# Low parts of stationary weights 64 bytes further than the activations, mod 512, in a two-layer decoder trunk

## The chip, the cores and the metric

One core of a Trainium2 chip. The metric is the device time of one execution in microseconds; the time given for a kernel is the median of its runs.

## What is computed

Two decoder layers over 256 tokens of width 2048, in float32. Layer 0 mixes with stick-breaking attention, layer 1 with forgetting attention (softmax with cumulative log-forget-gate bias); each has 16 heads of 128, and 4 heads that attend to a memory of 256 vectors. Nearly all arithmetic is in the projections and the feed-forward:

```python
for i in range(DEPTH):                       # DEPTH = 2
    h = _rmsnorm(x, attn_norm[i])
    mem_h = _rmsnorm(mem, mem_norm[i])
    # q, k, v, q_mem = split(h @ w_in); attention; memory attention (mem_h @ w_mem_kv)
    # y = concatenate([o, o_mem]) @ w_out
    x = x + y
    x = x + _conv_ffn(_rmsnorm(x, ffn_norm[i]), ffn_w_up[i], ffn_conv_w[i], ffn_conv_b[i], ffn_w_down[i])
return _rmsnorm(x, final_norm)

def _conv_ffn(h, w_up, conv_w, conv_b, w_down):
    u = h @ w_up                             # 2048 -> 2 * 5632
    # causal depthwise conv of width 3, then split into gate and val
    return (jax.nn.silu(gate) * val) @ w_down
```

## The kernel before

**Splitting.** Activations and weights are float32. Each is split into a high part (rounded to the type `float32r`) and a low part (the rest), and a product is summed from three: high x high, high x low, low x high. Activations are kept transposed, features on partitions, as tiles `xg` (inputs of a block) and `s` (slots for hidden features and heads), 128 x 512: columns 0 to 255 hold the high part of the 256 tokens, 256 to 511 the low part.

**Weights.** They come from memory in chunks of 128 x 1024 (896 in some of the down projection) into one of seven tiles `raw`, issued by the queue SP. `split_chunk` then makes two tiles: `wh`, a cast on ScalarE, and `wl`, the difference `raw - wh` on VectorE. Three pairs of `wh` and `wl` are used in turn (`AHEAD` = 2 chunks ahead of TensorE). `stream` hands out the next chunk's pair and starts later loads and splits.

**Two kinds of jobs.** In a weights-stationary job (`col_job`, and `project` through `colmm`) the weights are loaded into the array, 128 columns at a time, and the activations move through. For each 128 x 128 block of weights that is a wide product, `wh` stationary with all 512 columns of the activation moving (high x high and low x high in one), and a narrow one, `wl` stationary with the 256 high columns:

```python
self.mm(ps, wh[:, s], x, start and i == 0, last)
self.mm(ps[:, :T], wl[:, s], x[:, :T], False, last)
```

Queries, keys, the output projections and the whole feed-forward run so. In a weights-moving job (`row_job`, for values) the activations are stationary and 512 columns of `wh` or `wl` move; `mm3` issues three wide products there.

In the trace a product is written out<-moving,stationary: `acc<-xg,wl` is the narrow product with the low part stationary, `acc<-wh,xg` a weights-moving one. Each matmul has its own weight load, shown on PEld with the same names.

**Order.** The engines' orders are those in which the code issues (class `Ordered`): background work (norms, attention, gates) is cut into steps that `tick` runs after every four weight blocks.

**Places.** `place` puts a blank tile `pad` of 1920 bytes first, so that `xg` begins at byte 18432 of each partition; all tiles of `xg`, `memk`, `memv`, `wh`, `wl`, `s`, `v` begin at a multiple of 512 bytes. So do the 128-column blocks in them (512 bytes each). Constants behind them lie otherwise: `negL`, the triangle of the stick-breaking sums, at 480 mod 512.

Of the kernel before, what the change touches and what calls it, by code (L numbers as in the profile page):

```python
# [7 lines left out]
F32 = mybir.dt.float32  # L8
F32R = mybir.dt.float32r
# [5 lines left out]
P = 128  # L15
# [6 lines left out]
CW = 1024  # L22
SPARE = 7
AHEAD = 2
RAW = 7


# [19 lines left out]
class Ordered:  # L47


    def __init__(self, tc, engine):  # L50
        self.tc, self.engine, self.last = tc, engine, None
# [31 lines left out]
class Trunk:  # L83
# [9 lines left out]
    def __init__(self, ctx, tc, a, out, chunks):  # L93
        self.a, self.out = a, out
        self.KT = a["xT"].shape[1]
        self.NH = a["wq0"].shape[0]
        self.NF = a["wg0"].shape[0]
        self.chunks, self.dry = (chunks, False) if chunks is not None else ([], True)
        if self.dry:
            no = Nothing()  # L100
            self.sp = self.act = self.dve = self.pool = self.pe = no
            self.cp = self.rawp = self.wp = self.padp = self.bigp = self.slots = no
            self.pairp = self.vp = self.sm = self.rp = self.acc = self.zp = self.misc = no
        else:
            nc = tc.nc
            self.sp, self.act, self.dve, self.pool, self.pe = (
                Ordered(tc, e) for e in (nc.sync, nc.scalar, nc.vector, nc.gpsimd, nc.tensor))
            pool = lambda n, b, **k: ctx.enter_context(tc.tile_pool(name=n, bufs=b, **k))
            psum = dict(space=bass.MemoryType.PSUM)
            self.padp = pool("pad", 1)  # L110
            self.bigp = pool("big", 1)
            self.wp = pool("w", 1)
            self.slots = pool("slots", MH + max(self.NH, self.KT) + SPARE)
            self.vp = pool("v", 1)
            self.pairp = pool("pair", 3)
            self.rawp = pool("raw", RAW)
            self.cp = pool("const", 1)
            self.sm = pool("small", 2)
            self.rp = pool("rp", 2)
            self.acc = pool("acc", 4, **psum)  # L120
            self.zp = pool("zp", 1, **psum)
            self.misc = pool("misc", 2, **psum)
        self.n = 0
        self.bg = []
        self.chunk = self.loaded = self.copied = 0
        self.raws, self.ws, self.subs = {}, {}, []
# [137 lines left out]

    def weight(self, name, i):

        return self.wp.tile([P, CW], F32R, tag=f"{name}{i % (AHEAD + 1)}", name=self.nm(name))

    def split_chunk(self, i, pieces=1):

        raw = self.raws.pop(i)
        n = raw.shape[-1]
        wh, wl = self.weight("wh", i)[:, :n], self.weight("wl", i)[:, :n]

        def low(s=slice(0, n)):
            self.dve.tensor_tensor(out=wl[:, s], in0=raw[:, s], in1=wh[:, s].bitcast(F32), op=ALU.subtract)

        if pieces == 1:
            self.act.copy(wh, raw)
            self.subs.append(low)  # L280
        for j in range(pieces if pieces > 1 else 0):
            s = slice(j * n // pieces, (j + 1) * n // pieces)
            self.act.copy(wh[:, s], raw[:, s])
            low(s)
        self.ws[i] = (wh, wl)

    def stream(self, src):

        if self.dry:
            self.chunks.append(src)  # L290
            return Nothing(), Nothing()
        i = self.chunk
        self.chunk += 1
        last = len(self.chunks)
        last_load = min(i + AHEAD + RAW, self.loaded + 2, last)
        while self.loaded < last_load:
            self.load_chunk(self.loaded)
            self.loaded += 1
        while self.copied < min(i + AHEAD + 1, last):
            self.split_chunk(self.copied)  # L300
            self.copied += 1
        return self.ws.pop(i)
# [36 lines left out]
    def row_job(self, src, acts, before=None):  # L339

        nch = src.shape[0]
        for c in range(nch):
            wh, wl = self.stream(src[c])
            if before:
                before(c + 2)
            if c == 0:
                pss = [self.acc_bank() for _ in range(2)]
            for i in range(2):
                x = acts[2 * c + i]
                s = slice(i * 512, (i + 1) * 512)  # L350
                for b in range(2):
                    self.mm3(pss[b], x[:, b * P:(b + 1) * P], x[:, T + b * P:T + (b + 1) * P],
                             wh[:, s], wl[:, s], c == i == 0, c == nch - 1 and i == 1)
                self.tick()
        return pss
# [538 lines left out]

    def place(self):

        self.blank("pad", 1920)

    def blank(self, tag, size):

        if not self.dry:
            t = self.padp.tile([P, size // 4], F32, tag=tag, name=tag)
            self.pool.memset(t[:, :1], 0.0)

    def run(self):
# [31 lines left out]
@with_exitstack  # L937
def trunk_kernel(ctx, tc, arrays, out):
    order = Trunk(ctx, tc, arrays, out, None)
    order.run()  # L940
    Trunk(ctx, tc, arrays, out, order.chunks).run()


def pack(i):
# [75 lines left out]
```

## Time and profile before

| | us |
|---|---|
| median of 3 runs | 2515.45 (2515.24 to 2516.77) |
| profiled execution, its own time | 2517.73 |
| its span | 2516.0 |
| TensorE matmuls busy (PE) | 2490.8 (99%) |
| weight loads busy (PEld) | 2159.9 (86%) |
| VectorE busy (DVE) | 1767.2 (70%) |
| ScalarE busy (ACT) | 1360.9 (54%) |
| GpSimd busy (POOL) | 120.0 (5%) |

Time outside the span is 1.7 us. Matmuls are pipelined: a row's duration reaches from its start to its end in the array and overlaps the next one's, so TensorE's pace is read from the starts. A weight load overlaps the matmul beside which it stands.

### The profile page before, as it was taken

The page shows a single profiled execution, that of the slowest core. Times are in us where ns is not written, and L with a number is a line of the kernel's source. Part 1 is how long each engine was busy: PE and PEld are TensorE (multiplying, and loading weights), DVE is VectorE, ACT ScalarE, POOL GpSimd, SP SyncE. Part 2 cuts the span into 40 slices and gives each one's busy share as a digit, 9 for nine tenths or more (in the row PEclk, how much of TensorE's full clock was granted, in tenths as well). Part 3 has the DMA queues.
Part 4 walks back from the last instruction along what each step waited for, and adds up shares of the span by engine and source line. Part 5 has one row for each costly group of instructions (what it writes and reads, how often), then busy time and mean ns, then how long its engine had stood idle before and what let it go on. Part 6 is the DMA issues. An engine that isn't in the chain of part 4 may idle for free.

```text
span 2516.0 us, 36772 instructions
## 1 busy us (share of the span) xinstructions
PE 2490.8 (99%) x14048; PEld 2159.9 (86%) x14048; DVE 1767.2 (70%) x2598; ACT 1360.9 (54%) x1993; POOL 120.0 (5%) x153
## 2 busy tenths in 40 slices
PE   8999999999999999999999999999999999999998
PEld 6888888888888888888888888888888888888887
DVE  8756666677766776677776666666777667767776
ACT  5646665456544554465565444545655446544554
POOL 7200000100000000000100000001000000000000
PEclk9999999999999999999999999999999999999999
DMA  7565554555555566655665555455555655565553
GB/s 267 159 190 165 173 161 150 187 183 187 188 182 188 186 189 183 190 187 177 196 202 163 183 174 162 158 168 184 185 188 185 184 192 188 183 183 190 187 178 128
DMA packets 129920, 456.00 MB, mean 181 GB/s; under 512 B 14544, under 2 KB 15056, under 8 KB 129744
## 3 DMA queue, kind: packets, MB, share of 16 engines
q1 hardware_dynamic: 129168, 453.17, 56.9%
q8 instruction: 110, 1.80, 0.3%
q10 hardware_dynamic: 576, 0.48, 0.1%
q14 instruction: 66, 0.54, 0.1%
HBM read 451.50 MB, written 2.10 MB: 180 GB/s over the span
## 4 chain that ended last, share of the span: by engine, by line
PE 67%; issue 30%; DVE 1%; ACT 1%; DMA 1%; SPq 0%; POOLq 0%; DVEq 0%; POOL 0%; ACTq 0%
PE acc L57 63%; PE zp L57 2%; PE misc L57 1%; DVE s L57 0%; DVE wl L57 0%; DVE xg L57 0%; DMA raw<-in_wv 0%; ACT wh L57 0%; ACT L57 0%; DVE x L57 0%; DMA raw<-in_wk 0%; ACT s L57 0%; DMA raw<-in_wmk 0%; SPq L57 0%; ACT p L57 0%
## 5 line engine op out<-in xcount | busy, mean ns | idle before, releaser
L57 PE MATMUL acc<-xg,wh 128*128 128x512 f32 x3968 | 1407.6, 400 | 0.0
L57 DVE TENSOR_TENSOR wl<-raw,wh 128x1024 fp32r<-128x1024 f32 (+2 forms) x866 | 1047.6, 1210 | 373.8 <-ACT wh L57 359.5
L57 ACT CAST wh<-raw 128x1024 fp32r<-128x1024 f32 (+2 forms) x866 | 894.5, 1033 | 656.4 <-PE acc L57 626.9
L57 PE MATMUL acc<-xg,wl 128*128 128x256 f32 x3968 | 1116.8, 281 | 1.1 <-DVE wl L57 0.9
L57 PEld LDWEIGHTS acc<-xg,wh 128*128 128x128 f32 x3968 | 748.1, 189 | 182.6 <-DVE xg L57 0.6
L57 PE MATMUL acc<-s,wh 128*128 128x512 f32 x2190 | 770.6, 398 | 0.0
L57 PEld LDWEIGHTS acc<-xg,wl 128*128 128x128 f32 x3968 | 752.7, 190 | 2.7 <-DVE wl L57 2.4
L57 PE MATMUL acc<-s,wl 128*128 128x256 f32 x2176 | 611.8, 281 | 0.0
L57 PEld LDWEIGHTS acc<-s,wh 128*128 128x128 f32 x2190 | 411.0, 188 | 99.8
L57 PEld LDWEIGHTS acc<-s,wl 128*128 128x128 f32 x2176 | 411.9, 189 | 0.0
L57 ACT COPY s<-acc 128x256 f32<-128x256 f32 x256 | 94.9, 372 | 350.2 <-PE acc L57 349.9
L57 DVE TENSOR_TENSOR s<-acc,s 128x256 f32<-128x256 f32 x256 | 108.6, 424 | 238.3 <-ACT s L57 238.3
L57 DVE SCALAR_TENSOR_TENSOR s<-s,convw,s 128x255 f32<-128x255 f32 x352 | 169.2, 481 | 6.3
L57 PE MATMUL acc<-wh,xg 128*128 128x512 f32 x512 | 164.9, 397 | 6.0 <-ACT wh L57 6.0
L57 POOL TENSOR_TENSOR ssq<-ssq,s 128x256 f32<-128x256 f32 x75 | 72.3, 964 | 1339.2 <-issue 1078.5
L57 DVE TENSOR_TENSOR x<-acc,x 128x256 f32<-128x256 f32 x255 | 107.3, 423 | 38.2 <-PE acc L57 33.7
L57 PEld LDWEIGHTS acc<-wh,xg 128*128 128x128 f32 x512 | 97.6, 191 | 26.1 <-ACT wh L57 6.0
L57 DVE TENSOR_TENSOR s<-s,s 128x256 f32<-128x256 f32 (+1 forms) x254 | 108.8, 429 | 8.4 <-ACT s L57 5.3
L57 ACT ACTIVATE s<-s,convb,convw 128x256 f32<-128x256 f32 x176 | 106.0, 603 | 2.6 <-DVE s L57 1.5
L57 PE MATMUL acc<-wl,xg 128*128 128x512 f32 x256 | 101.7, 397 | 2.0 <-DVE wl L57 2.0
L57 DVE TENSOR_TENSOR s<-s,rB 128x256 f32<-128x256 f32 x208 | 89.2, 429 | 7.2
L57 ACT CAST s<-s 128x256 fp32r<-128x256 f32 x164 | 66.6, 407 | 32.4 <-DVE s L57 32.2
(119 smaller groups left out, 895.3 us busy)
## 6 DMA issues: line engine op xcount, KB each, us to landing
raw<-in_wg SPq DMA_DIRECT2D x176, 512.0 KB, 3.8
raw<-in_wu SPq DMA_DIRECT2D x176, 512.0 KB, 3.8
raw<-in_wd SPq DMA_DIRECT2D x128, 448.0 KB, 3.3
raw<-in_wq SPq DMA_DIRECT2D x64, 512.0 KB, 3.8
raw<-in_wk SPq DMA_DIRECT2D x64, 512.0 KB, 4.0
raw<-in_wo SPq DMA_DIRECT2D x64, 512.0 KB, 4.0
raw<-in_wd SPq DMA_DIRECT2D x64, 512.0 KB, 3.5
raw<-in_wv SPq DMA_DIRECT2D x63, 512.0 KB, 3.5
```

The lines of the kernel that those rows point to most:

```text
L57: r = op(*args, **kwargs)
```

## The change

The low parts' tiles get 16 more elements (64 bytes), and a blank tile of 448 bytes is put behind each pair, so that pairs stay a multiple of 512 bytes apart. In weights-stationary jobs the low part is written to, and read from, the tile at an offset of 16 elements; in weights-moving jobs (`row_job` tells `stream` so, and the dry run that lists the chunks remembers them in `moving`) at offset 0. The high parts keep offset 0 in all jobs. `wh`, `wl` and the blank tiles are touched once in order, at the start, to fix their places.

```diff
+SHIFT = 16
...
     def weight(self, name, i):
 
-        return self.wp.tile([P, CW], F32R, tag=f"{name}{i % (AHEAD + 1)}", name=self.nm(name))
+        return self.wp.tile([P, CW + (SHIFT if name == "wl" else 0)], F32R, tag=f"{name}{i % (AHEAD + 1)}",
+                            name=self.nm(name))
+
+    def shift(self, i):
+
+        return 0 if i in self.moving else SHIFT
...
-        wh, wl = self.weight("wh", i)[:, :n], self.weight("wl", i)[:, :n]
+        wh, wl = self.weight("wh", i)[:, :n], self.weight("wl", i)[:, self.shift(i):self.shift(i) + n]
...
-    def stream(self, src):
+    def stream(self, src, moving=False):
 
         if self.dry:
+            if moving:
+                self.moving.add(len(self.chunks))
             self.chunks.append(src)
...
-            wh, wl = self.stream(src[c])
+            wh, wl = self.stream(src[c], True)
...
     def place(self):
 
-        self.blank("pad", 1920)
-
-    def blank(self, tag, size):
+        self.blank(self.padp, "pad", 1920)
+        for i in range(AHEAD + 1):
+            for name in ("wh", "wl"):
+                t = self.weight(name, i)
+                if not self.dry:
+                    self.pool.memset(t[:, :1].bitcast(F32), 0.0)
+            self.blank(self.wp, f"gap{i}", 512 - 4 * SHIFT)
+
+    def blank(self, pool, tag, size):
```

Places in the built programs, bytes of a partition: before, `wh` at 83968, 92160, 100352 and `wl` at 88064, 96256, 104448; after, `wh` at 83968, 92672, 101376 and `wl` at 88064, 96768, 105472 (all 0 mod 512), read from 64 bytes further in weights-stationary jobs. All later tiles move up by 1536 bytes.

TensorE, ScalarE and SP issue the same instructions in the same order. On GpSimd nine memsets of one column are added. Its first rows before, from the blank tile on:

```order
L57 MEMSET pad 128x1
L57 MEMSET mhalf 128x2
L57 MEMSET ones 128x128
L57 MEMSET ident 128x128
L57 ISA
L57 AFFINE_SELECT ident<-ident 128x128
```

and after:

```order
L58 MEMSET pad 128x1
L58 MEMSET wh_96 128x1
L58 MEMSET wl_98 128x1
L58 MEMSET gap_100 128x1
L58 MEMSET wh_102 128x1
L58 MEMSET wl_104 128x1
L58 MEMSET gap_106 128x1
L58 MEMSET wh_108 128x1
L58 MEMSET wl_110 128x1
L58 MEMSET gap_112 128x1
L58 MEMSET mhalf 128x2
L58 MEMSET ones 128x128
```

The constants `mhalf`, `ones` and `ident` now come behind the nine.

## Rows read from the trace of the kernel before

**Rows 1.** Page, part 1: busy us (share of the span), instructions, each engine.

```profile
PE 2490.8 (99%) x14048; PEld 2159.9 (86%) x14048; DVE 1767.2 (70%) x2598; ACT 1360.9 (54%) x1993; POOL 120.0 (5%) x153
```

**Rows 2.** Waits of TensorE: who for whom, us in total, times, longest.

```profile
PE acc L57 <- ACT wh L57: 6.0, 1, 6.0
PE acc L57 <- DVE wl L57: 2.9, 8, 0.6
```

**Rows 3.** Groups by shape, TensorE: out<-moving,stationary, shapes, count, busy us, mean ns.

```profile
L57 PE MATMUL acc<-xg,wl 128*128 128x256 f32 x3968 | 1116.8, 281 | 1.1 <-DVE wl L57 0.9
...
L57 PE MATMUL acc<-s,wl 128*128 128x256 f32 x2176 | 611.8, 281 | 0.0
L57 PE MATMUL acc<-wh,xg 128*128 128x512 f32 x512 | 164.9, 397 | 6.0 <-ACT wh L57 6.0
```

**Rows 4.** Windows, feed-forward of layer 0: stretch, us, busy (count) by engine, clock, DMA.

```profile
530.00:1260.00 730.00, 730.00 (x4134) 633.44 (x4133) 541.22 (x811) 395.59 (x558) 11.00 (x13) 1.00 0.60 186
```

**Rows 5.** Timeline, TensorE, weights-moving job to weights-stationary one: start us, duration us.

```profile
162.24 0.61 PE L57 MATMUL acc<-wh,xg 128*128 128x512 f32 x2
...
163.60 0.39 PE L57 MATMUL acc<-wh,xg 128*128 128x512 f32 x1
163.83 0.39 PE L57 MATMUL acc<-xg,wh 128*128 128x512 f32 x1
164.05 0.28 PE L57 MATMUL acc<-xg,wl 128*128 128x256 f32 x1
```

**Rows 6.** Timeline, TensorE, steady weights-stationary run.

```profile
599.84 0.40 PE L57 MATMUL acc<-xg,wh 128*128 128x512 f32 x1
600.07 0.28 PE L57 MATMUL acc<-xg,wl 128*128 128x256 f32 x1
600.19 0.40 PE L57 MATMUL acc<-xg,wh 128*128 128x512 f32 x1
600.42 0.28 PE L57 MATMUL acc<-xg,wl 128*128 128x256 f32 x1
600.54 0.40 PE L57 MATMUL acc<-xg,wh 128*128 128x512 f32 x1
600.78 0.28 PE L57 MATMUL acc<-xg,wl 128*128 128x256 f32 x1
600.90 0.40 PE L57 MATMUL acc<-xg,wh 128*128 128x512 f32 x1
```

**Rows 7.** Timeline, weight loads in the same run.

```profile
600.42 0.19 PEld L57 LDWEIGHTS acc<-xg,wh 128*128 128x128 f32 x1
600.54 0.19 PEld L57 LDWEIGHTS acc<-xg,wl 128*128 128x128 f32 x1
```

**Rows 8.** Timeline, TensorE: negL loaded under a wide product.

```profile
230.36 0.40 PE L57 MATMUL acc<-wh,xg 128*128 128x512 f32 x1
230.59 0.34 PE L57 MATMUL zp<-p,negL 128*128 128x384 f32 x1
```

**Rows 9.** Timeline, TensorE: negL loaded under a narrow product.

```profile
204.42 0.28 PE L57 MATMUL acc<-xg,wl 128*128 128x256 f32 x1
204.54 0.33 PE L57 MATMUL zp<-p,negL 128*128 128x384 f32 x1
```

**Rows 10.** Timeline, TensorE: a short narrow interval.

```profile
404.09 0.28 PE L57 MATMUL acc<-s,wl 128*128 128x256 f32 x1
404.20 0.40 PE L57 MATMUL acc<-s,wh 128*128 128x512 f32 x1
```

**Rows 11.** Timeline, GpSimd, the first memsets.

```profile
0.80 0.10 POOL L57 MEMSET pad<- 128x1 f32 x1 [0.29 <-POOLq L1009]
0.83 0.10 POOL L57 MEMSET mhalf<- 128x2 f32 x1
```

**Rows 12.** Timeline, GpSimd, its first square; in brackets its idle time ahead.

```profile
4.40 0.61 POOL L57 TENSOR_TENSOR ssq<-x 128x256 f32<-128x256 f32 x1 [2.82 <-DMA x<-in_xT]
```

**Rows 13.** Groups by shape, VectorE: the split's low part.

```profile
L57 DVE TENSOR_TENSOR wl<-raw,wh 128x1024 fp32r<-128x1024 f32 x734 | 904.4, 1232 | 258.8 <-ACT wh L57 244.6
```

More of the change, by code (lines that the diff above doesn't have):

```diff
@@ L97, in __init__ @@
         self.NF = a["wg0"].shape[0]
-        self.chunks, self.dry = (chunks, False) if chunks is not None else ([], True)
+        self.chunks, self.moving, self.dry = (*chunks, False) if chunks is not None else ([], set(), True)
         if self.dry:
@@ L895, in place @@
     def place(self):
-        self.blank("pad", 1920)
-    def blank(self, tag, size):
+        self.blank(self.padp, "pad", 1920)
[6 more added lines that the diff above has]
+    def blank(self, pool, tag, size):
         if not self.dry:
-            t = self.padp.tile([P, size // 4], F32, tag=tag, name=tag)
+            t = pool.tile([P, size // 4], F32, tag=tag, name=tag)
             self.pool.memset(t[:, :1], 0.0)
@@ L940, in trunk_kernel @@
     order.run()
-    Trunk(ctx, tc, arrays, out, order.chunks).run()
+    Trunk(ctx, tc, arrays, out, (order.chunks, order.moving)).run()
 def pack(i):
```

## The prediction

> **What bounds the kernel now.** I read the page's busy line first: TensorE's matmuls cover 2490.8 of 2516.0 us, and in the stretch of rows 4 the granted clock is 1.00, its upper level of 2.4 GHz [rows 1, 4]. That alone says little, since pipelined matmuls count as busy however slowly they follow one another. So the second view is TensorE's waits: 6.0 us for the first high parts at the start, 2.9 us for low parts, and a few smaller ones [rows 2]. TensorE waits for nobody; the span is the sum of the intervals between matmul starts, and whatever shortens an interval shortens the span.
>
> Which intervals? The groups by shape show 3968 + 2176 = 6144 low-part products of 256 columns, each with a high-part product of 512 columns beside it [rows 3]. These are the weights-stationary jobs. A window with nothing else in it, 730.00 us of the first feed-forward, holds 4134 matmuls [rows 4]: 2 x 730.00 / 4134 = 353.2 ns for a pair. 6144 x 0.3532 = 2170 us, 86% of the span. The mean duration in rows 3 (281 ns) is no interval: such durations overlap and must not be summed; only start to start counts.
>
> In a pair the wide product takes 0.23 to 0.24 us to the next start, the narrow one about 0.12 us [rows 6]: three wide ones sum to 0.70 us, 233 ns each to within some 3 ns, as starts are rounded to 10. I take 235 and, from the pair, 118 for the narrow one. Each matmul starts together with the load of the weights that the next one uses [rows 6, 7]: under the wide product runs the load of the low part, under the narrow one the load of the next high part. So a low part's address is read by the load while the activations' 512 columns are being read.
>
> Does the wide product have to take 235 ns? In the weights-moving jobs it doesn't: from 162.24 to 163.83 us seven products of 512 columns start, 1.59 / 7 = 227 ns each, with a load of 128 columns under each as well, and all operands at a multiple of 512 bytes there too. The first wide product of the weights-stationary job that follows starts at 163.83 and the next matmul at 164.05: about 0.22 us. In the steady run the wide ones take 0.23 to 0.24 [rows 5, 6]. Same line, same shapes, same places mod 512; what differs is what ran just ahead, a wide product or a narrow one whose load fills nearly all of its 118 ns. I read this as a meeting of two readers, the one of the moving columns and the one of the weights, whose price depends on how far one lags the other when a product begins. That the price exists is shown; that it goes by address is my inference.
>
> Few rows speak on addresses, and none on 64 bytes ahead. negL lies at 480 mod 512, 32 bytes behind the moving operand. Its load under a wide product makes an interval of 0.23 (230.36 to 230.59), where 227 is usual [rows 5, 8]. Under a narrow product negL's load makes 0.12 (204.42 to 204.54) as all others do [rows 9]. So 32 bytes backwards change an interval by less than the 10 ns to which the rows are rounded.
>
> **The change part by part.**
>
> *Low parts 64 bytes further.* It touches the load under the wide product in every pair, 6144 times. 64 bytes are 16 of the 512 columns, at 227 ns per 512 some 7.1 ns of the moving reader's way. If the meeting of the readers is put off by that much, a wide product gets 7.1 ns shorter; by this mechanism it can't get under the 227 ns of rows 5, which is 8 ns below the present 235. I take 7.1 ns: 6144 x 7.1 ns = 43.6 us. Ends: the best is a wide product at 227 and a narrow one at 0.11 us, the shortest that the rows show [rows 10], say 113 ns within its rounding: 340 a pair, 13.2 x 6144 = 81 us. The worst is the same step with the other sign, a reader that has to follow the load for one more piece of 64 bytes: the load of 128 columns lasts up to 0.12 us (600.42 to 600.54) [rows 7], the stream of 128 columns 227 / 4 = 57 ns [rows 5], so following costs about as much again as the piece itself, 7.1 ns, and 43.6 us for one piece, 349 us for all eight of a load.
>
> *High parts at the same place.* The load under the narrow product keeps its addresses; the narrow interval changes only through the lag that the wide one leaves behind. I price it at nothing, with +-4 ns a pair (0.11 to 0.12 us) [rows 6, 10], 25 us either way, inside the ends above.
>
> *Weights-moving jobs.* They use shift 0, so the products with wh or wl moving, x512 in the largest group [rows 3], keep their places. Nothing.
>
> *Larger tiles and gaps.* A slot of low parts grows by 64 bytes, a gap of 448 follows each: 3 x 512 = 1536 bytes, so every later tile moves by a multiple of 512 and keeps its place mod 512. Nothing.
>
> *Nine more memsets on GpSimd* at the start: they follow each other at 0.80 and 0.83, so 9 x 0.035 = 0.3 us ahead of mhalf, ones and ident [rows 11]. GpSimd then idles 2.82 us before its first square, for x to land, and takes it up at 4.40 [rows 12]; all nine memsets lie before 1.2 us, long before TensorE's first product, which waits 6.0 us for the weights' cast [rows 2]. Hidden; without that idle time it would be 0.3 us.
>
> *Splitting.* VectorE writes the low part at an offset of 64 bytes in the same shape, 1232 ns for a chunk of 1024 [rows 13]; a chunk lasts eight pairs, 2.83 us, and at the forecast 8 x 346 = 2.77 us. The split still fits twice, and TensorE's 2.9 us of waiting on low parts [rows 2] may grow by a microsecond or two. So a shorter pair isn't taken by the next stage.
>
> Sum: -43.6 us, against the profiled execution's 2517.73 us: 2474.1. It was 2.3 us above the median 2515.45, so the forecast for the median is 2515.45 - 43.6 = 2471.9, rounded to 2472.
>
> **The rivals.**
>
> *A. The place doesn't matter.* Then pairs stay at 353.2 and the time at 2515. For it: negL, 32 bytes behind, is loaded at the cost of any other within 10 ns, under a wide product and under a narrow one [rows 8, 9]. Against it: the 227 and 235 ns of rows 5 and 6 at equal places, which shows that load and stream do touch. It is also how the change could fail to do what it says: the weights lie elsewhere, but only the lag in time counts.
> On this the Trainium skill has a rule, in TensorE: Matmul & The Clock Gate, Part 2, on LDWEIGHTS: the array has two independent SBUF read ports, so loading the next weights takes no read bandwidth from the running matmul. By it the sum would be nothing, 2515 us. The trace doesn't bear it out in full, since equal products with equal loads take 227 and 235 ns [rows 5, 6].
>
> *B. The other side: the readers lock.* The moving reader finishes its first 64 bytes and comes upon the piece that the load has just begun; being the faster one it has to follow the load instead of meeting it late. Place: each wide product. Price: 7.1 ns for each piece that it follows, worked out above: one piece gives 2515 + 43.6 = 2559 us, all eight 2515 + 349 = 2864. It decides from the point at which the load begins less than 16 columns (7.1 ns) behind the stream. For it: the load's row starts within 10 ns of the matmul's [rows 6, 7]. Against it: the wide products come out longer behind a narrow one, which I read as a load that lags by more than that.
>
> *C. The whole excess goes.* Wide at 227, narrow at 113, 2515 - 81 = 2434 us. For it: both values occur in the rows [rows 5, 10]. Against it: the loads under the narrow ones stay where they are.
>
> **How the numbers follow.** Forecast 0.55 (2440 to 2505), C or better 0.09, A 0.14, B 0.22. About 0.2%, 5 us, is what a measurement of this kernel can tell from no change. Faster: 0.55 + 0.09 = 0.64; same 0.14; slower 0.22. The range starts at 2434 less a little, 2430, leaving out 0.06 of C, and ends at 2560, which takes in A and B with one piece, half of B: some 0.11 is left out above.
>
> **What would show it.** Right: pairs of 344 to 349 ns in the feed-forward window, with the wide product near 228 and the narrow one near 118, weights-moving products still at 227 and TensorE's waits still under 20 us in all. A shows as 353 unchanged. B shows as wide products of 245 ns or more. What would make it wrong though the wide product does get shorter: a narrow product that grows by as much, because the load of the next high part now starts against a stream that is ahead; then the pair stays and the time with it.

## The result and the profile after

The changed kernel's median is 2481.93 us (2479.63 to 2482.32, four runs) against 2515.34 for the kernel before (2514.95 to 2516.77, four runs): a ratio of 0.9864, 95% interval 0.9847 to 0.9881. The median fell by 33.4 us; between the two profiled executions it is 2517.73 - 2479.63 = 38.1 us.

TensorE still sets the end. The busy line of the page after the change (before: [rows 1]):

```profile
PE 2450.2 (99%) x14048; PEld 2156.3 (87%) x14048; DVE 1768.1 (71%) x2598; ACT 1367.7 (55%) x1993; POOL 120.6 (5%) x162
```

Same counts, and nine more on GpSimd. TensorE's two largest waits for weights after (who for whom, us in total, times, longest; before: [rows 2]):

```profile
PE acc L58 <- ACT wh L58: 6.0, 1, 6.0
PE acc L58 <- DVE wl L58: 3.3, 9, 0.6
```

So the gain isn't in waits. It is in the pace of the pairs. The window inside layer 0's feed-forward after (stretch, us, busy and count by engine, clock, DMA; before: [rows 4]):

```profile
530.00:1240.00 710.00, 710.00 (x4098) 627.83 (x4097) 534.75 (x799) 392.89 (x548) 11.16 (x13) 1.00 0.60 190
```

2 x 710.00 / 4098 = 346.5 ns for a pair, where it was 353.2; 6.7 ns less. The steady run, TensorE's timeline after (start us, duration us; before: [rows 6]):

```profile
599.71 0.39 PE L58 MATMUL acc<-xg,wh 128*128 128x512 f32 x1
599.94 0.28 PE L58 MATMUL acc<-xg,wl 128*128 128x256 f32 x1
600.06 0.39 PE L58 MATMUL acc<-xg,wh 128*128 128x512 f32 x1
600.29 0.28 PE L58 MATMUL acc<-xg,wl 128*128 128x256 f32 x1
600.40 0.39 PE L58 MATMUL acc<-xg,wh 128*128 128x512 f32 x1
```

The interval of 0.24 is rarer and the durations of wide products are 0.39 instead of 0.40. Rounded starts don't say more; from the starts of all wide and narrow products of the two traces in nanoseconds (intervals over 270 ns left out) the wide interval's mean fell from 235.9 to 229.6 and the narrow one's stayed (117.1 and 117.2). In the feed-forward of the kernel before these means hide a cycle of three pairs, 350, 361 and 349 ns long, whose wide products take 233, 241 and 236 ns in turn; in the changed kernel pairs take 345 to 348 ns. The weights-moving jobs stayed at 227 ns in the mean; in the one below seven wide products start from 160.63 to 162.21, 226 ns each (before: [rows 5]).

```profile
160.63 0.62 PE L58 MATMUL acc<-wh,xg 128*128 128x512 f32 x2
161.08 0.39 PE L58 MATMUL acc<-wl,xg 128*128 128x512 f32 x1
161.31 0.62 PE L58 MATMUL acc<-wh,xg 128*128 128x512 f32 x2
161.76 0.39 PE L58 MATMUL acc<-wl,xg 128*128 128x512 f32 x1
161.99 0.39 PE L58 MATMUL acc<-wh,xg 128*128 128x512 f32 x1
162.21 0.39 PE L58 MATMUL acc<-xg,wh 128*128 128x512 f32 x1
```

6.3 ns less on a wide product and 0.1 more on a narrow one make 6.2 ns x 6144 = 38 us, the whole difference of the spans (2516.0 - 2477.6 = 38.4). Where the time went is settled; why 64 bytes do it is what the experiments are for.

### The profile page after: what moved, and what is told of

The parts are those of the page before. It is cut to its first block, busy times and chain, and to the rows that moved or that the text cites. A ratio compares the mean times of both kernels' runs of the same rounds, so it can differ in the third digit from the quotient of the medians.

```text
span 2477.6 us, 36782 instructions
## 1 busy us (share of the span) xinstructions
PE 2450.2 (99%) x14048; PEld 2156.3 (87%) x14048; DVE 1768.1 (71%) x2598; ACT 1367.7 (55%) x1993; POOL 120.6 (5%) x162
## 4 chain that ended last, share of the span: by engine, by line
PE 66%; issue 30%; DVE 2%; ACT 1%; DMA 1%; SPq 0%; POOLq 0%; DVEq 0%; POOL 0%; ACTq 0%
PE acc L58 63%; PE zp L58 2%; PE misc L58 1%; DVE wl L58 1%; DVE xg L58 1%; DVE s L58 0%; ACT wh L58 0%; DVE x L58 0%; DMA raw<-in_wv 0%; ACT L58 0%; ACT s L58 0%; DMA raw<-in_wk 0%; DMA raw<-in_wmk 0%; SPq L58 0%; ACT p L58 0%
## 5 line engine op out<-in xcount | busy, mean ns | idle before, releaser
L58 PE MATMUL acc<-xg,wh 128*128 128x512 f32 x3968 | 1381.4, 392 | 0.5 <-DVE xg L58 0.5
L58 PE MATMUL acc<-s,wh 128*128 128x512 f32 x2190 | 756.9, 391 | 0.0
```

Source lines behind the costliest of these rows:

```text
L58: r = op(*args, **kwargs)
```

## Experiments

In the table a pair's length is 2 x (length of the window) / (matmuls in it), in 600 to 1200 us (layer 0's feed-forward) and in 1850 to 2400 us (layer 1's); a window's count takes in a matmul or two at its ends, so that a pair reads 0.2 ns short: from the starts the paces are 340.0, 346.7, 350.0 and 353.3 ns. Places are those of the load against the moving activations, mod 512, in weights-stationary jobs. Times of single executions have no interval, and since one set of places can have more than one pace (e1 below), a row shows a pace that was found there and not the only one. The kernel before beside them took 2515.57 (one execution), 2516.7 and 2516.27 (medians of 13 each) in the groups of e1, e2, e3 and e7, of e4, e5, e6 and e1b, and of e9 to e12.

| kernel | low | high | pair, layer 0 | pair, layer 1 | time us |
|---|---|---|---|---|---|
| before | 0 | 0 | 353.1 | 353.1 | 2515.34 |
| changed | 64 | 0 | 346.5 | 346.5 | 2481.93 |
| e1 | 0 | 0 | 353.1 | 346.5 | 2503.65 (one) |
| e1b, the same again | 0 | 0 | 353.1 | 353.0 | 2516.54 |
| e6, all tiles at 64 | 0 | 0 | 353.1 | 353.1 | 2517.31 (one) |
| e10 | 32 | 0 | 346.4 | 346.5 | 2478.94 (one) |
| e2 | 128 | 0 | 346.5 | 346.5 | 2483.25 (one) |
| e9 | 256 | 0 | 353.1 | 353.1 | 2517.24 (one) |
| e3 | 448 | 0 | 349.8 | 349.9 | 2502.09 (one) |
| e11 | 0 | 64 | 339.9 | 349.8 | 2471.89 (one) |
| e5 | 64 | 64 | 353.1 | 353.0 | 2524.36 (one) |
| e4 | 128 | 64 | 349.8 | 349.8 | 2504.6 (one) |
| e12 | 64 | 448 | 353.3 | 353.1 | 2501.04 |
| e7, another order | 0 | 0 | 348.3 | 348.3 | 2489.87 (one) |

The two windows, TensorE alone, before:

```profile
600.00:1200.00 600.00, 600.00 (x3398) 1.00 0.59 186
1850.00:2400.00 550.00, 550.00 (x3115) 1.00 0.59 186
```

and after:

```profile
600.00:1200.00 600.00, 600.00 (x3463) 1.00 0.59 189
1850.00:2400.00 550.00, 550.00 (x3175) 1.00 0.59 189
```

In the experiments' kernels `SHIFT` is replaced by two offsets in elements of 4 bytes, `LOW` and `HIGH`, which hold in weights-stationary jobs, and tiles and gaps are sized by them. The diffs show the lines that matter, against the changed kernel where nothing else is said.

**e1: the changed layout without the offset.** Gaps of 512 bytes, the same memsets, low parts at offset 0.

```diff
-SHIFT = 16
+LOW = 0
+HIGH = 0
...
-            self.blank(self.wp, f"gap{i}", 512 - 4 * SHIFT)
+            self.blank(self.wp, f"gap{i}", 512)
```

> All tiles lie where the change puts them to within 64 bytes (gaps of 512 bytes behind each pair, later tiles 1536 bytes further, the nine memsets), but low parts start at 0 mod 512 in all jobs. Place theory (what counts is where the load reads against the activations, mod 512): wide interval back at 236 ns, pair 353, time 2515 us. Layout theory (the gaps or the other tiles' new places did it): wide 230, pair 347, 2482 us.

It ran in 2503.65 us, between the kernel before and the changed one. The two windows of its one execution show why:

```profile
600.00:1200.00 600.00, 600.00 (x3398) 1.00 0.59 186
1850.00:2400.00 550.00, 550.00 (x3175) 1.00 0.59 190
```

353.1 ns in layer 0, 346.5 in layer 1, with the same code line, the same shapes and the same places mod 512. This neither theory had: at equal places two paces are steady, and the job in layer 1 ran at the faster one without any offset. Whether the layout had a part in it was then asked by running the same kernel again.

**e1b: the same kernel, ten executions.**

> The kernel of e1 (gaps, no shift) once more, several executions: it ran layer 0's feed-forward at 353.3 and layer 1's at 346.7 ns. Entry theory (at equal places both rhythms are steady, and which one a job falls into is set by what ran ahead to the nanosecond): executions or profiles may differ by steps of up to 25 us, between 2482 and 2515, and the profile may show another mix. Place theory (the other places mod 2048 in this kernel decide): the same mix and 2503 us each time.

Eight of the ten took 2515 to 2518 us, two 2504.5 and 2504.3. The kernel before, in 13 executions beside it, had the same two groups of times: eleven at 2514.7 to 2518.3, two at 2504.7 and 2503.1; in another group of 13 two at 2500.7 and 2501.4. The ratio of the two kernels is 0.9999 (0.9978 to 1.0019). The execution profiled this time:

```profile
600.00:1200.00 600.00, 600.00 (x3398) 1.00 0.55 186
1850.00:2400.00 550.00, 550.00 (x3116) 1.00 0.55 186
```

So the layout is worth nothing, and the 12 us of e1 were the other pace of one feed-forward: from 1775 to 2490 us the kernel before has 4049 matmuls, 2024 pairs, and 6.6 ns each are 13 us. Which pace a run falls into at equal places differs between executions of one and the same kernel, as the two profiles show. That the four fast executions of the kernel before had one feed-forward at the faster pace fits their times and is not shown: none of them was profiled. Chance of this kind doesn't explain the change: the lowest of all executions of the kernel before is 2500.70 us, the highest of the changed kernel 2482.32.

**e2, e9, e3, e10: other distances of the low part.** The same edit with another number (for e3 112 elements, which is 64 bytes behind, mod 512), and a gap that keeps pairs a multiple of 512 bytes apart:

```diff
-SHIFT = 16
+LOW = 32     # e2; 64 in e9, 112 in e3, 8 in e10
+HIGH = 0
...
-            self.blank(self.wp, f"gap{i}", 512 - 4 * SHIFT)
+            self.blank(self.wp, f"gap{i}", 384)     # e2; 256 in e9, 64 in e3, 480 in e10
```

> Low parts 128 bytes further instead of 64. Put-off theory (each 64 bytes put the meeting of load and stream off by one more step of 7 ns, down to the 227 ns of the weights-moving jobs): wide 227 ns, pair 344 to 345, about 2465 us. Equal-place theory (only an equal place is dear, any other is as good as 64): wide 230, pair 347, 2482 us. Lock theory (too far ahead the stream runs into the load and follows it): wide over 240, above 2530 us.

> Low parts 448 bytes further, that is 64 bytes behind the activations mod 512. Put-off theory: the meeting comes one step earlier or lasts one piece longer, wide 243 ns, pair 360, about 2555 us. Equal-place theory: wide 230, pair 347, 2482 us. If the sign doesn't count at all because the period isn't 512: 2515 us.

> Low parts 256 bytes further, half of the period. Rhythm theory with a safe zone ahead of the equal place (64 and 128 gave 346.7, 448 gave 350.0): at 256 346.7 or one of the other steady values, 2482 to 2515 us. Lock theory (the stream catches up with a load that begins well ahead and has to follow it): wide over 240, above 2530 us.

> Low parts 32 bytes further. If the step that counts is 64 bytes and the stream reads in such pieces: as at the equal place, 353.3 and 346.7 mixed, 2500 to 2515 us. If any lead over the equal place opens the good rhythm: 346.7, 2482 us. If the lead counts in proportion: about 350, 2498 us.

128 bytes: 346.5 ns, no further gain, which is against the put-off theory. The window of e2:

```profile
600.00:1200.00 600.00, 600.00 (x3463) 1.00 0.60 189
```

448 bytes: 349.8, neither the 360 of the put-off theory nor the 346.5 of the equal-place theory:

```profile
600.00:1200.00 600.00, 600.00 (x3431) 1.00 0.59 187
```

256 bytes: as at the equal place, to the count of matmuls in both windows:

```profile
600.00:1200.00 600.00, 600.00 (x3398) 1.00 0.59 186
1850.00:2400.00 550.00, 550.00 (x3115) 1.00 0.59 186
```

That speaks for a pattern that repeats every 256 bytes, not 512; no run shows it for other places. The stream running into a load and following it, with wide products of 240 ns and more in the mean, was not seen in e9 nor anywhere. 32 bytes are as good as 64, so any of 32, 64 and 128 brought 346.5 in the feed-forwards (in layer 1's attention, 1270 to 1650 us, pairs took 349.2 from the starts in e2 and 346.8 in the changed kernel):

```profile
600.00:1200.00 600.00, 600.00 (x3464) 1.00 0.60 189
1850.00:2400.00 550.00, 550.00 (x3175) 1.00 0.60 189
```

From the starts in nanoseconds, in e10 that is an alternation of pairs of 340 and 353, in the changed kernel pairs of 345 to 348: the mean is what repeats.

**e6: everything 64 bytes further.**

Against the kernel before, beside the nine memsets less the three for gaps, which it doesn't have:

```diff
-        self.blank("pad", 1920)
+        self.blank(self.padp, "pad", 1984)
```

> The kernel before with the first blank tile 64 bytes larger: activations, low parts, high parts and all later tiles lie at 64 mod 512, so nothing changes between load and stream. Relative theory: as at equal places, pairs of 353.3 (or 346.7 where the run was entered otherwise), 2500 to 2515 us. Absolute theory (64 mod 512 is a good place for a load by itself): 346.7 throughout, 2482 us.

353.1 in both windows and 2517.31 us: the place of the tiles by itself brought nothing in this execution, so what counts is the place of the loads against the stream.

```profile
600.00:1200.00 600.00, 600.00 (x3398) 1.00 0.55 185
1850.00:2400.00 550.00, 550.00 (x3115) 1.00 0.55 186
```

**e5 and e4: both parts, at other places than their expectations name.** High parts at an offset of 64 bytes, in a tile that had grown by as much:

```diff
-SHIFT = 16
+LOW = 0     # e5; 16 in e4
+HIGH = 16
...
-        return self.wp.tile([P, CW + (SHIFT if name == "wl" else 0)], F32R, tag=f"{name}{i % (AHEAD + 1)}",
+        return self.wp.tile([P, CW + (LOW if name == "wl" else HIGH)], F32R, tag=f"{name}{i % (AHEAD + 1)}",
```

The low tiles stand behind the high ones, so they too began 64 bytes further: in e5 low and high parts both lay at 64 in weights-stationary jobs, in e4 the low ones at 128 and the high ones at 64, and in weights-moving jobs of both the low parts lay at 64 and the high ones at 0. The expectations go by low parts at 0 in e5 and at 64 in e4.

> Low and high parts both 64 bytes further in weights-stationary jobs. By now pairs are seen to run in steady rhythms: 353.3 or 346.7 ns at equal places, 346.7 at 64 and 128, 350.0 at 448. Rhythm theory (what matters is that the two loads of a pair lie differently against the stream, or that the load under the wide product is ahead): can't say which rhythm, but one of few fixed values. Put-off theory (each load gains by itself): narrow interval shorter too, 110 to 114, pair about 342, about 2450 us. If only the low part counts: 346.7, 2482 us.

> High parts 64 bytes further, low parts at the same place: the mirror image. Theory that the wide product's load is the one that counts: 353, 2515 us or, through the rhythm at equal places, anything between 2482 and 2515. Theory that the two loads need only differ in place: 346.7, 2482 us. Lock theory: the narrow product has to follow its load, 120 ns or more, 2530 us.

By the places that they had: with both at 64 the pair is back at 353.1, although the load under the wide product is as far ahead as in the change. That rules out that this load alone decides, and also that VectorE's writing the low part at 64 bytes does it, since it did so in e5 too. With 128 and 64 it is 349.8. Windows of e5 and e4:

```profile
600.00:1200.00 600.00, 600.00 (x3399) 1.00 0.54 186
```

```profile
600.00:1200.00 600.00, 600.00 (x3431) 1.00 0.55 187
```

These two runs also show why the change leaves weights-moving jobs alone. There the weights are the stream; with the low parts 64 bytes further, the load under their products reads 64 bytes behind. The timeline of e5:

```profile
160.78 0.40 PE L59 MATMUL acc<-wh,xg 128*128 128x512 f32 x1
161.01 0.40 PE L59 MATMUL acc<-wl,xg 128*128 128x512 f32 x1
...
163.80 0.39 PE L59 MATMUL acc<-wl,xg 128*128 128x512 f32 x1
164.03 0.39 PE L59 MATMUL acc<-wh,xg 128*128 128x512 f32 x1
164.26 0.40 PE L59 MATMUL acc<-xg,wh 128*128 128x512 f32 x1
```

15 wide products from 160.78 to 164.26, 232 ns each instead of 227; over the 960 wide products of such jobs 5 us. From the starts, products with high parts moving, from offset 0, take 232 as well as those with low parts, so here too it is not a product's own two places alone that set its price.

**e11: the mirror image.** High parts 64 bytes ahead in weights-stationary jobs, low parts at 0 in all; the high tile is 512 bytes larger.

```diff
-SHIFT = 16
+LOW = 0
+HIGH = 16
...
-        return self.wp.tile([P, CW + (SHIFT if name == "wl" else 0)], F32R, tag=f"{name}{i % (AHEAD + 1)}",
+        return self.wp.tile([P, CW + (LOW if name == "wl" else 128 if HIGH else 0)], F32R, tag=f"{name}{i % (AHEAD + 1)}",
...
-        wh, wl = self.weight("wh", i)[:, :n], self.weight("wl", i)[:, self.shift(i):self.shift(i) + n]
+        h, l = self.shift(i, HIGH), self.shift(i, LOW)
+        wh, wl = self.weight("wh", i)[:, h:h + n], self.weight("wl", i)[:, l:l + n]
```

> High parts 64 bytes further in weights-stationary jobs, low parts at the same place as the activations, weights-moving jobs as before (each high tile is 512 bytes larger so that the low tiles stay). Theory that only the load under the wide product must be ahead: 353.3, 2515 us. Theory that the two loads of a pair must lie differently: 346.7, 2482 us. With high and low both at 64 pairs ran at 353.3, so a lead of the high part seems to cost what that of the low part gains; by that sum the mirror is worse than equal places, 356 to 360, 2535 to 2560 us.

No theory had this: 2471.89 us in one execution, faster than the changed kernel. Its two feed-forwards differ:

```profile
600.00:1200.00 600.00, 600.00 (x3531) 1.00 0.62 193
1850.00:2400.00 550.00, 550.00 (x3145) 1.00 0.59 187
```

339.9 ns in layer 0, the 340 that the prediction had named as the best, and 349.8 in layer 1. Layer 0's timeline:

```profile
799.61 0.39 PE L59 MATMUL acc<-xg,wh 128*128 128x512 f32 x1
799.84 0.28 PE L59 MATMUL acc<-xg,wl 128*128 128x256 f32 x1
799.95 0.39 PE L59 MATMUL acc<-xg,wh 128*128 128x512 f32 x1
800.18 0.28 PE L59 MATMUL acc<-xg,wl 128*128 128x256 f32 x1
800.29 0.39 PE L59 MATMUL acc<-xg,wh 128*128 128x512 f32 x1
```

Each wide interval reads 0.23 and each narrow one 0.11, and wide products start 0.34 apart. The wide product has shortened although the load under it reads from the same place as before; only the load under the narrow one was moved. So a wide product's price doesn't hang on the load under it alone: the loads of a pair are to be looked at together.

**e12: low 64 ahead, high 64 behind.** As e11, with the high parts at 112 elements, the low ones at 16 and a gap of 448 bytes.

> Low parts 64 bytes ahead as in the change, high parts 64 bytes behind (448 mod 512). If a lead of the high part costs and a lag gains: narrow interval 113 to 115, pair 343, about 2460 us, better than the change. If the good rhythm of 346.7 is the floor for any places: 2482 us. If a lag costs as it does for the low part: 350, 2500 us.

Ten executions spread over 2487.41 to 2515.71, median 2501.04, ratio 0.9941 (0.9912 to 0.9969). The profiled one had 353.3 and 353.1 in the windows:

```profile
600.00:1200.00 600.00, 600.00 (x3397) 1.00 0.59 185
1850.00:2400.00 550.00, 550.00 (x3115) 1.00 0.59 186
```

Not better than the change, and again more than one pace at one set of places: in this trace, from the starts, the pairs from 416 to 518 us take 346.8 ns and those of the feed-forwards 353.3. The ten times fall into three groups, three at 2514.06 to 2515.71, four at 2500.56 to 2502.43 and three at 2487.41 to 2489.26, some 13 us apart, which is what one feed-forward at the faster pace is worth; only one of the slowest group was profiled, so that this is their reason is not shown.

**e7: another order at equal places.** Two wide products, then their two narrow ones, with `LOW` and `HIGH` at 0 and no gaps.

```diff
-            self.mm(ps[:, :T], wl[:, s], x[:, :T], False, last)
+            held.append((s, x, last))
+            if i % 2 or i == len(acts) - 1:
+                for s, x, last in held:
+                    self.mm(ps[:, :T], wl[:, s], x[:, :T], False, last)
+                held = []
```

> Low parts at 0 mod 512 as in the kernel before, but two wide products follow each other, then their two narrow ones. History theory (a wide product costs 227 ns behind a wide one and some 236 behind a narrow one, at equal places): the second wide product of each two takes 227, the first 236 or less; mean wide about 231, time about 2485 us if the narrow ones stay at 117. Theory that each wide product in a weights-stationary job is dear whatever ran before (its operands, not its predecessor): all wide at 236, 2515 us.

2489.87 us; a pair's share is 348.3 ns.

```profile
600.00:1200.00 600.00, 600.00 (x3445) 1.00 0.59 188
```

The time came out near the history theory's 2485, its reason did not: from the starts in nanoseconds a wide product behind a wide one takes 233.2 and one behind a narrow one 233.0. The predecessor's width doesn't set a product's price here; another order makes another steady pace.

## Why the prediction was right, and where its reason was not

**What bounds the kernel:** as read. TensorE waits 6.0 and 3.3 us for weights where it waited 6.0 and 2.9, and a shorter pair went into the time in full; the split on VectorE kept up.

**The size.** Forecast were 7.1 ns off the wide product, the narrow one unchanged, weights-moving jobs at 227 ns, and 346.1 ns a pair. Measured were 6.3 ns off the wide product, 0.1 more on the narrow one, 227 ns, and 346.5. The sum was 43.6 us and the profiled executions differ by 38.1. The term is a little too large; moreover in both layers' attention pairs were shorter than 353 already: from the starts 350.3 from 120 to 415 us and 351.7 from 1270 to 1650 us, against 346.8 in both after the change, so that less than 6.7 ns was to be had there.

**The step that failed** is the reason for the 7.1 ns: "If the meeting of the readers is put off by that much, a wide product gets 7.1 ns shorter." A lead that counts by its length would have given more at 128 bytes (e2: the same), less at 32 (e10: the same), and would have left the wide product alone when only the high part moves (e11: from the starts 226 to 227 ns in layer 0's feed-forward, where it was 236). What the runs show in its place: in a long run the pairs, wide and narrow in turn, settle into one of a few steady paces, 339.9, 346.5, 349.8 or 353.1 ns in the windows, steps of 3.3 or twice that (348.3 in the order of e7). Which paces were found depends on where both loads lie against the stream, and where there is more than one, the one that a run falls into differs between stretches of one execution (e1, e11, e12) and between executions (e1 and e1b). At the change's places 346.5 was found in both layers of its one profile, and its four executions lie within 2.7 us. So, as far as these executions show, the change replaced a pair of places with two paces, mostly the slower, by one with the faster; that 7.1 ns lie near the step of 6.7 ns is chance, and with it that the forecast of 2472 us came so near.

**The reading of rows 5 and 6** was half right. Equal products at equal places do cost 227 or up to 241 ns; that what runs just ahead decides it (a narrow product) is refuted by e7, and in the trace of before itself by the cycle of 233, 241 and 236 ns, all behind narrow products. The 0.12 us that the prediction gives a load is the distance of two loads' starts in rows 7; the rows themselves last 0.19 us and overlap. The first wide product of the job at 163.83 was short because the run had not yet settled, which is my reading and not shown by a run of its own.

**Nothing for the larger tiles, gaps and memsets:** right, by e1b's ratio of 0.9999.

**Rival A, the place doesn't matter:** wrong as it stands. With nothing changed in the weights-stationary jobs but the place of the low parts, a pair of layer 0's feed-forward takes 339.9 (e11) or 353.1 ns (e5). The Trainium skill's rule (TensorE: Matmul & The Clock Gate, Part 2, on LDWEIGHTS) is that the weights' read port is independent of the stream's and that loading takes no read bandwidth from a running matmul. These numbers speak against drawing from it that the place is free; whether it is bandwidth that load and stream take from each other, no run here shows. negL's rows, rounded to 10 ns, could not have shown a step of 6.7. But A's core, that the lag in time counts, may have its share: e1 had the fast pace without any offset. **Rival B, the lock:** not seen at any place tried; no feed-forward ran slower than that of the kernel before (353.3 ns from the starts). A slower kernel exists (e5, 2524.36 us), mostly through its weights-moving jobs. **Rival C:** its 340 ns exist, at other places than those of the change: e11 moved the loads under the narrow products, which the change leaves where they are.

**What stays open:** what sets the steady paces inside the chip, and which event at a job's start chooses between them. If all weights-stationary jobs at e11's places ran at 339.9, that would be worth 6.6 ns x 6144 = 41 us more than the change, an estimate from its layer 0; its one execution was 10 us faster than the changed kernel, and how its executions spread was not measured.

## What to carry to other kernels

When TensorE is the bound and waits for nobody, measure start to start, not durations, and compare the same product in several places of the program: a difference of a few per cent at equal shapes can mean that loads and streams disturb each other, and moving one operand by 32 to 128 bytes is a cheap trial. Try the stationary operands one by one and together, since leads don't add up (64 and 64 gave 353.1, as 0 and 0). And profile more than one execution, because the same addresses can run at two paces; a gain of half a per cent in one execution (e1's 12 us) may be the other pace.

## What the runs showed of the hardware

Places of the weights' loads against the moving operand, in float32r, change a pair of products of 512 and 256 columns between 339.9 and 353.1 ns, at a granted clock of 1.00 in all windows above. In one execution each, an offset of 256 bytes on the low parts acted as none (e9, 353.1 ns), and so did one common to all operands (e6, 353.1 ns). At equal places two paces are steady within one execution, 353.1 and 346.5 ns (e1); that this is what spreads the executions of the kernel before from 2500.7 to 2518.3 us fits the step of 13 us for one feed-forward and is not shown.
